# A two-layer decoder trunk: block-inversion products in four runs, bonus sums behind the scores, branch outputs by sequence halves

## The chip, the cores and the metric

The kernel runs on one core of a Trainium2 chip. The metric is the device time of one execution in microseconds (us). Five engines of the core run side by side and meet through semaphores: PE (the matrix engine, TensorE; PEld are its weight loads), DVE (VectorE), ACT (ScalarE), POOL (GpSimd) and SP (SyncE, which issues the DMAs). Each works through its own instructions in the order of the program.

## The reference

Two layers over 1024 tokens of 1024 channels, then a final RMS norm. Each layer does this, in float32:

```python
h = rms_norm(x, norm_g) * (1.0 + scale) + shift        # shift, scale, gate from c
proj = h @ w_in                                         # 1024 -> 8320 columns
pool_u, pool_g, q, k, v, ret_g, rw, rw_g, gate_logits = split(proj)
o_pool = causal_pool_mixer(pool_u, ...) * silu(pool_g)  # windows 2, 4, 8, 16
o_ret  = retention(q, k, v, positions, ...) * silu(ret_g)   # 4 heads, rotary
o_rwkv = rwkv7_time_mix(rw, ...) * silu(rw_g)           # 8 heads of 64, delta rule
y = einsum('btnw,nwd->btnd', stack(o_pool, o_ret, o_rwkv), w_branch)
merged = sum(sigmoid(gate_logits) * y, axis=n)
x = x + gate * (merged @ w_out)
```

The RWKV mixer ends with `y = y + bonus`, where `bonus = sum(r * k * r_k) * v` within a head of 64 channels.

## The kernel before

Activations lie with channels on the 128 partitions and tokens along the free axis, in two halves of 512 tokens. Every large product is made in three matmuls of a reduced-precision float type: each operand x is split into a high part (a copy rounded by ACT, line 562) and a low part (x minus the high part, on POOL, line 563), and `mm3` adds hi·hi, lo·hi and hi·lo into one PSUM tile `acc`. There are three `acc` buffers, two further PSUM buffers of the tag `mx` for all small products, and a double-width PSUM tile `two`.

The weights come as items: `k`, `r`, `v`, `pu`, `rq`, `gate`, `br` (the branch projection), `wg`, `out` and so on. `plan_layer` yields the items in the order in which PE takes them; for each, `wprep` loads two weight tiles `wr` and splits them into `wh` and `wl`. After every dense matmul, `mm1` calls `pump`, which advances the lanes of side work (`norm`, `post`, `rwkv`, `mix`, `ada`) that are due by a clock kept while the program is built: `clock[0]` counts PE's time, `idle_at` the other engines', and a task yields how long it wants to wait. So the place of each small product among the dense ones is settled when the program is built.

One RWKV task (`rwkv_task`) handles two heads on 128 partitions; there are four in a layer, eight in all, and each is called a head here. Its steps:

- `prepare(h)` for each half: decay and key terms (small products `lw`, `nps`), the operand tiles AR and BK, the transposes `vt` of the values into Z, and the bonus: `rkh` and `rkl` are the high and low parts of r·k·r_k, `bon` is their sum over the head by a product with a block matrix of ones, and `bv` is `bon` times v (line 881). `bon` is in a `mx` buffer, which is free again when DVE has formed `bv`.
- `scores(h)`: the transposes `bt` of BK, then the score products `g` (one head in `mx`, one in `two`), masked by DVE into the tile G (line 904).
- `states` and `invert` side by side: the products `av`, and the inversion of 32x32 triangular blocks by forward substitution on DVE, which begins with two transposes (line 928).
- Products of 32x32 blocks that join two inverted blocks into one of 64x64: `m1` and `m2`, each for two quarters q of the units, 16 products a time. Each stands in the profile as 32 matmuls named `m`. They wait for a time by the planner's clock, and between them stand `pace()` and `until(left[q])`.
- Sixteen chunk steps, then a norm; `rwkv_post` writes the result to `od` in DRAM.

Retention (`ret_task`) and pooling (`pool_task`) write their outputs to `od` too. The gate tiles `gsg` that come early are evicted by ACT into tiles of the tag `mo` and stored in `gd`. The rope tables are made once, beside the first head: each half loads the positions, DVE reduces the angle in 12 steps, and ACT takes two sines (lines 299, 300).

The merge: `load_o(n)` loads the outputs of branch n (eight tiles `ol`) and splits them into the single tile `oG` (high parts) and eight tiles `olo` of the tag `mi` (low parts). The tag G of `oG` has one buffer, so the load of a branch waits until the matmuls of the branch before have read theirs. Each `br` item needs all of its branch's tiles; its four products are evicted by DVE and added by DVE or POOL (`mrg`).

Of the kernel before, what the change touches and what calls it, by code (L numbers as in the profile page):

```python
# [19 lines left out]
T = 1024  # L20
# [46 lines left out]
def GT(n, *ds):  # L67
    return [("gate", n, d) for d in ds]


def BR(n, *ds):
    return [("br", n, d) for d in ds]
# [24 lines left out]
def trunk_kernel(ctx, tc, xT, cvec, pos, vecs, consts, w_ada, w_all, pool_w, lora_w, out):  # L97
# [24 lines left out]
    def slot(tag, n, w=HF):  # L122
        def f(s, dt=F32):
            return tp.tile([P, w], dt, tag=tag, name=nm(s), bufs=n)

        return f

    t_rk = slot("rk", 4)
    t_lt = slot("lt", 4)
    t_ri = slot("ri", 7)  # L130
    t_mi = slot("mi", 8, HF + 16)
    t_mo = slot("mo", 4, HF + 16)
    t_vp = slot("vp", 2)
# [134 lines left out]
    def rope_tables():  # L268
        yield 15000
        MAGIC = 12582912.0  # L270
        TWO_PI = 2.0 * math.pi
        cw, left = [], TWO_PI
        for _ in range(3):
            e = 2.0 ** (math.frexp(left)[1] - 8)
            cw.append(math.floor(left / e) * e)
            left -= cw[-1]
        cw.append(left)
        PI_F = 3.1415925
        for h in range(2):
            s = slice(h * HF, (h + 1) * HF)  # L280
            pi = t_mo("posi", I32)[:, 0:HF]
            tc.keep_in_program_order(nc.sync.dma_start(out=pi, in_=pos[:, s].to_broadcast([P, HF])))
            ang = mo("ang")
            nc.vector.tensor_copy(ang, pi)
            nc.vector.tensor_scalar_mul(ang, ang, cs("freq"))
            n = mo("nrot")
            for big in (4096.0, 1.0):
                nc.vector.tensor_scalar(n, ang, 1.0 / (TWO_PI * big), MAGIC, op0=ALU.mult, op1=ALU.add)
                nc.vector.tensor_scalar_sub(n, n, MAGIC)
                for cc in cw:  # L290
                    nc.vector.scalar_tensor_tensor(ang, n, -cc * big, ang, op0=ALU.mult, op1=ALU.add)
                yield 6000
            m = mo("over")
            nc.vector.tensor_scalar_add(n, ang, math.pi / 2)
            nc.vector.tensor_scalar(m, n, math.pi, -TWO_PI, op0=ALU.is_gt, op1=ALU.mult)
            nc.vector.tensor_tensor(n, n, m, op=ALU.add)
            for a in (n, ang):
                nc.vector.tensor_scalar(a, a, PI_F, -PI_F, op0=ALU.min, op1=ALU.max)
            nc.scalar.activation(n[0:64, :], n[0:64, :], AF.Sin)
# [171 lines left out]
    def plan_layer(l):  # L471
        yield from [("lora",)] + RW(0)
        pools = deque(PL(i) for i in range(4))
        pre = deque(GT(0, *range(8)) + GT(1, 0, 1, 4, 5, 6, 7) + GT(2, 2, 3, 4, 5, 6, 7, 0, 1) + GT(1, 2, 3))
        late = deque([("wg", 0), ("wg", 1), ("wg", 2)])
        done = 0
        while done < 4 or prog.get((l, 3), 0) < 13 or pools or halves[l] < 15:
            if done < 4 and prog.get((l, done), -1) >= 0:
                done += 1
                if done < 4:  # L480
                    yield from RW(done)
                yield from RT(done - 1)
            elif pools and 4 - len(pools) <= done and len(lanes["mix"]) < 2:
                yield from pools.popleft()
            elif pre or late:
                q = late if late and (done == 4 and prog.get((l, 3), -1) >= 0 or not pre) else pre
                it = q.popleft()
                early[l].add(it)
                yield it
            elif pools:  # L490
                yield from pools.popleft()
            elif done < 4:
                done += 1
                if done < 4:
                    yield from RW(done)
                yield from RT(done - 1)
            else:
                break
        yield ("merge",)
        seq = GT(1, 2, 3) + BR(0, 0, 2, 4, 6) + [("wg", 0), ("wg", 1)]  # L500
        seq += GT(1, 0, 1) + BR(1, 0, 2) + GT(1, 4, 5) + BR(1, 4)
        seq += [("wg", 2), ("wg", 3)] + GT(1, 6, 7) + BR(1, 6)
        seq += GT(2, 0, 1) + BR(2, 0) + GT(2, 2, 3) + BR(2, 2) + GT(2, 4, 5, 6, 7) + BR(2, 4, 6)
        yield from [it for it in seq if it not in early[l]]
        for part in range(2 + (l + 1 == L)):
            yield from [("out", d, part) for d in out_order(l, part)]
# [276 lines left out]
    def rwkv_task(l, hp, kT, rT, vp, lt, lw):  # L783
# [14 lines left out]
        bvs = []  # L798

        def prepare(h):  # L800
            cr = slice(8 * h, 8 * h + 8)
# [69 lines left out]
            for par in range(2):  # L871
# [1 line left out]
                    Z[64:128, 8 * h + par : 8 * h + 8 : 2, :],  # L873
                    ps[64 * par : 64 * par + 64, :].rearrange("p (c n) -> p c n", n=P),
                )
            yield wait(rkh, rkl)
            ps = mx("bon")
            mmul(ps, bone, rkh, start=True, stop=False)
            mmul(ps, bone, rkl, start=False, stop=True)
            bv = t_ri("bv")  # L880
            nc.vector.scalar_tensor_tensor(bv, ps, 0.5, vp[h], op0=ALU.mult, op1=ALU.mult)
            bvs.append(bv)
# [3 lines left out]
        def scores(h):  # L886
            yield until(whole[h] + 1000)
            for q in range(2):
                ps = mx("bt")
                c0 = 8 * h + 4 * q  # L890
                for c in range(4):
                    trans(ps[:, c * P : (c + 1) * P], jt(BK, slice(0, P), c0 + c), timed=True)
                nc.scalar.copy(BKt[:, c0 : c0 + 4, :], ps.rearrange("p (c n) -> p c n", n=P))
                yield 1300
            for q in range(2):
                c0 = 8 * h + 4 * q
                gps = [mx("g"), cyt()]
                for j in range(4):
                    for hd in range(2):
                        rows = slice(64 * hd, 64 * hd + 64)  # L900
                        mmul(gps[hd][:, j * P : (j + 1) * P], jt(BK, rows, c0 + j), jt(AR, rows, c0 + j), timed=True)
                for hd in range(2):
                    u0 = 16 * hd + c0
                    nc.vector.tensor_tensor(
                        G[:, u0 : u0 + 4, :], gps[hd].rearrange("p (u n) -> p u n", n=P), rm, op=ALU.mult
                    )
                yield 2600
        yield from prepare(0)
        yield from side(scores(0), prepare(1))
        yield from scores(1)  # L910
# [62 lines left out]
        for q in range(2):  # L973
# [4 lines left out]
            nc.scalar.copy(T1[32:64, q * HF : (q + 1) * HF], ps[32:64, :])  # L978
            left.append(max(whole[1], at(MT)) + 300)
            if q == 0:  # L980
                yield pace()
                back(0)
        for q in range(2):
            yield until(left[q])
            ps = mx("m2")
            for u in range(16):
                uu = 16 * q + u
# [428 lines left out]
    for l in range(L):  # L1416
# [39 lines left out]
        merged = None  # L1456
        gates = {}

        def split_o(G, row, kt, o, h):
            hi = G[:, kt * T + h * HF : kt * T + (h + 1) * HF].bitcast(F32R)  # L1460
            lo = mi("olo").bitcast(F32R)
            split(o, hi, lo)
            row.append((hi, lo))

        def new_o():
            return gtile("oG")

        def load_o(n, res):
            G = new_o()
            for kt in range(4):  # L1470
                row = []
                res.append(row)
                for h in range(2):
                    o = mo("ol")
                    nc.sync.dma_start(out=o, in_=od[l][n, kt, h])
                    split_o(G, row, kt, o, h)
                    yield 1250

        gs_free = [t_ri] * 7 + [t_rk] * 4 + [t_vp] * 2 + [t_cs] * 2
        gs_used = {}  # L1480

        def gate_tile(key):
# [16 lines left out]
        def next_o(n):  # L1499
            nonlocal otask  # L1500
            if n < 3:
                osplit.append([])
                otask = add("norm", load_o(n, osplit[n]))

        osplit = []
        unsplit = deque()
        otask = None
        next_o(0)
        mt = [r8("mrg") for _ in range(4)]
        merged = [[None, None] for _ in range(8)]  # L1510
        while wready[0][0][0] != "out":
# [11 lines left out]
            else:  # L1523
                n, d0 = it[1], it[2]
                assert brs.popleft() == (n, d0)
                finish("norm", otask)
                dh = [(d, h) for d in (d0, d0 + 1) for h in range(2)]
                if n == 2 and d0 == 6:
                    dh = [(d, h) for h in range(2) for d in (d0, d0 + 1)]
                for d, h in dh:  # L1530
                    ps = acc_ps()
                    mm3(ps, ws[d - d0], [osplit[n][k][h] for k in range(4)], True, True)
# [12 lines left out]
                    while unsplit and gleft[l] == 0:  # L1545
# [4 lines left out]
                if d0 == 6:  # L1550
                    next_o(n + 1)
        if l:
            drain("ada")
        for task in gate_ada:
# [160 lines left out]
```

## Time and profile before

| | before |
|---|---|
| time, median of 3 runs (lowest to highest) | 2431.59 us (2431.26 to 2433.96) |
| span of the profiled execution | 2431.3 us |
| DVE, ACT, POOL busy | 54%, 33%, 34% |
| DMA over the span | 218.29 MB in queue q1, 28.5% of 16 engines |
| matmuls of the tile m | 1024 of 13312 |

The profiled execution is one execution. Its own time is its span, 2431.3 us from the first to the last instruction; the three runs lie from 0.04 below to 2.7 us above it. In the views of waits a row names the engine and tile that waited, the line, and whose result ended the wait. In timelines a row gives the start, the time from the first start to the last end, and the number of equal instructions; a dense matmul (128x512) lasts 0.39 us there, but in a steady stream one starts every 0.23 us.

### The profile page before, as it was taken

To read this page: it belongs to the slowest core of one execution; us is meant where nothing else is said; L and a number is where in the kernel's file an instruction comes from. 1 tells how busy PE (TensorE), PEld (TensorE's weight loads), DVE (VectorE), ACT (ScalarE), POOL (GpSimd) and SP (SyncE) were. 2 spreads that over 40 slices of the span, in tenths; PEclk is the share of its full clock that TensorE was granted. 3 is DMA by queue.
4 is the path that set the end of the run, shared out by engine and by line. 5 is a ranking of instruction groups with operands and counts; after the bars stand their busy time and mean duration, and the time that the engine had idled before them with its cause. 6 is when DMAs were issued, how large, how long until landed. Compare 5 with 4: busy or idle time off the path is not lost. (4 is left out here: it accounts for less than half of the span.)

```text
span 2431.3 us, 34768 instructions
## 1 busy us (share of the span) xinstructions
PE 2353.2 (97%) x13312; PEld 1925.5 (79%) x13312; DVE 1313.5 (54%) x2564; ACT 799.9 (33%) x1481; POOL 820.8 (34%) x729
## 2 busy tenths in 40 slices
PE   5989999999999999999999999999999999999998
PEld 4768878878887888777877887888787888878888
DVE  7665477367468542457455646745644674322244
ACT  5542333333234223112453324323322323212243
POOL 4321232232232424364442222323313332455241
PEclk9999999999999999999999999999999999999999
DMA  7132112111213225666431211211211222543152
GB/s 252 49 109 70 40 40 75 53 39 53 67 52 109 75 70 173 190 202 206 153 114 44 79 40 40 83 37 44 67 58 39 67 73 71 186 130 96 52 152 79
DMA packets 122487, 220.51 MB, mean 91 GB/s; under 512 B 13904, under 2 KB 17232, under 8 KB 122320
## 3 DMA queue, kind: packets, MB, share of 16 engines
q1 hardware_dynamic: 122320, 218.29, 28.5%
q8 instruction: 104, 1.70, 0.3%
q14 instruction: 63, 0.52, 0.1%
HBM read 172.89 MB, written 45.35 MB: 90 GB/s over the span
## 5 line engine op out<-in xcount | busy, mean ns | idle before, releaser
L563 POOL TENSOR_TENSOR wl<-wr,wh 128x512 fp32r<-128x512 f32 x342 | 452.5, 1324 | 1150.8 <-ACT wh L562 1082.0
L445 PE MATMUL acc<-hhi,wh 128*128 128x512 f32 x2000 | 808.6, 404 | 9.6 <-ACT gsg L1150 8.2
L445 PE MATMUL acc<-hhi,wl 128*128 128x512 f32 x2000 | 811.4, 406 | 1.5 <-POOL r L1070 1.5
L445 PE MATMUL acc<-hlo,wh 128*128 128x512 f32 x2000 | 809.6, 405 | 0.0
L445 PEld LDWEIGHTS acc<-hhi,wh 128*128 128x128 f32 x2000 | 380.6, 190 | 78.9 <-ACT gsg L1150 9.4
L445 PEld LDWEIGHTS acc<-hhi,wl 128*128 128x128 f32 x2000 | 380.8, 190 | 70.5 <-POOL r L1070 2.0
L445 PEld LDWEIGHTS acc<-hlo,wh 128*128 128x128 f32 x2000 | 380.7, 190 | 66.1 <-issue 0.7
L562 ACT CAST wh<-wr 128x512 fp32r<-128x512 f32 x342 | 211.8, 620 | 619.2 <-PE acc L445 436.4
L445 PE MATMUL acc<-olo,wh 128*128 128x512 f32 x384 | 155.3, 405 | 5.9 <-POOL olo L563 5.9
L445 PE MATMUL acc<-oG,wh 128*128 128x512 f32 x384 | 155.0, 405 | 3.1 <-ACT oG L562 1.7
L445 PE MATMUL acc<-oG,wl 128*128 128x512 f32 x384 | 153.0, 400 | 0.0
L1032 DVE SCALAR_TENSOR_TENSOR S<-ch,pc,SP 64x64 f32<-64x64 f32 x256 | 72.5, 283 | 98.8 <-PE ch L445 96.1
L1020 DVE TENSOR_TENSOR xst<-two,MT 64x128 f32<-64x128 f32 x128 | 37.6, 293 | 157.8 <-PE two L445 143.8
L1008 ACT ACTIVATE SP<-S,pc 128x128 f32<-128x128 f32 x128 | 51.5, 402 | 208.1 <-DVE S L1032 198.0
L445 PEld LDWEIGHTS acc<-olo,wh 128*128 128x128 f32 x384 | 73.9, 192 | 25.3 <-POOL olo L563 8.9
L445 PEld LDWEIGHTS acc<-oG,wh 128*128 128x128 f32 x384 | 73.4, 191 | 22.8 <-ACT oG L562 2.9
L445 PEld LDWEIGHTS acc<-oG,wl 128*128 128x128 f32 x384 | 73.8, 192 | 17.8
L1539 DVE SCALAR_TENSOR_TENSOR gs<-gs,acc 128x512 f32<-128x512 f32 x64 | 43.5, 683 | 78.5 <-PE acc L445 78.5
L939 DVE TENSOR_TENSOR tm<-MT,two 64x30 f32<-64x30 f32 (+14 forms) x240 | 76.5, 319 | 12.9 <-ACT two L932 5.6
L945 DVE TENSOR_TENSOR two<-two,tm 64x30 f32<-64x30 f32 (+14 forms) x240 | 78.9, 329 | 7.3
L1027 DVE COPY Z<-ch 64x128 f32<-64x128 f32 x128 | 36.0, 282 | 82.1 <-PE ch L445 81.6
L1537 DVE SCALAR_TENSOR_TENSOR mrg<-gs,acc 128x512 f32<-128x512 f32 x32 | 22.0, 687 | 107.6 <-PE acc L445 105.4
(287 smaller groups left out, 3690.7 us busy)
## 6 DMA issues: line engine op xcount, KB each, us to landing
wr<-in_w_all SPq DMA_DIRECT2D x364, 256.0 KB, 2.7
gd<-gsg SPq DMA_DIRECT2D x74, 256.0 KB, 2.0
gs<-gd SPq DMA_DIRECT2D x74, 256.0 KB, 2.9
wada<-in_w_ada SPq DMA_DIRECT2D x70, 256.0 KB, 3.2
ol<-od SPq DMA_DIRECT2D x64, 256.0 KB, 3.0
ringG<-in_w_ada SPq DMA_DIRECT2D x26, 256.0 KB, 4.9
x<-in_xT SPq DMA_DIRECT2D x16, 256.0 KB, 4.8
od<-po SPq DMA_DIRECT2D x16, 256.0 KB, 2.0
```

Source lines behind the costliest of these rows:

```text
L445: return nc.tensor.matmul(out, lhsT=lhsT, rhs=rhs, start=start, stop=stop, **kw)
L562: nc.scalar.copy(hi, src)
L563: eng.tensor_tensor(lo, src, hi.bitcast(F32), op=ALU.subtract)
L939: nc.vector.tensor_tensor(pr, L3[:, i + 1 :, i : i + 1].to_broadcast([64, n, i]), M3[:, i : i + 1, 0:i].to_broadcast([64, n, i]), op=ALU.mult,
L945: nc.vector.tensor_tensor(M3[:, i + 1 :, 0:i], M3[:, i + 1 :, 0:i], pr, op=ALU.add)
L1008: nc.scalar.activation(SP, S, AF.Copy, scale=pcc)
L1020: nc.vector.tensor_tensor(xst[0:64, :], cy[64:128, 0:P], AV[:, c * P : (c + 1) * P], op=ALU.add)
L1027: nc.vector.tensor_copy(Z[0:64, c, :], ch[0:64, 0:P])
L1032: nc.vector.scalar_tensor_tensor(Sn[rw, rw], ch[rw, P + 64 * hd : P + 64 * hd + 64], pc[rw, c : c + 1], SP[rw, rw], op0=ALU.mult, op1=ALU.add,
L1537: nc.vector.scalar_tensor_tensor(m, s, 1.0, ps, op0=ALU.add, op1=ALU.mult)
L1539: nc.vector.scalar_tensor_tensor(s, s, 1.0, ps, op0=ALU.add, op1=ALU.mult)
```

## The change

Five edits:

1. The block-inversion products: at least 1500 ns of the planner's clock pass before the second, third and fourth run of 16 products.
2. The bonus: `bon` and `bv` leave `prepare(h)` and become a step of their own at the end of `scores(h)`.
3. The branch outputs are loaded and split by halves of the sequence. Half 0 of branch 0 and half 1 of branch 1 go into 8 tiles of the tag `ri`, half 1 of branch 0 and half 0 of branch 2 into 8 of `mi`, the other two into G. Three halves are asked for as the merge begins, the others when an earlier half has been used; each `br` item now does half 0 of both column tiles first.
4. `ri` has 14 buffers instead of 7 (one fewer goes to gate tiles), the rope tables use it instead of `mo`, and the scratch of dynamic DMAs is set to 1024 to make room.
5. The items wg 2 and wg 3, where they were not taken early, move ahead in the merge.

```diff
-    t_ri = slot("ri", 7)
+    t_ri = slot("ri", 14)
...
-            pi = t_mo("posi", I32)[:, 0:HF]
+            pi = t_ri("posi", I32)
...
-            ang = mo("ang")
+            ang = t_ri("ang")
...
-            n = mo("nrot")
+            n = t_ri("nrot")
...
-            m = mo("over")
+            m = t_ri("over")
...
-        seq += GT(1, 0, 1) + BR(1, 0, 2) + GT(1, 4, 5) + BR(1, 4)
-        seq += [("wg", 2), ("wg", 3)] + GT(1, 6, 7) + BR(1, 6)
+        seq += GT(1, 0, 1) + BR(1, 0) + [("wg", 2), ("wg", 3)] + BR(1, 2) + GT(1, 4, 5) + BR(1, 4)
+        seq += GT(1, 6, 7) + BR(1, 6)
...
-            yield wait(rkh, rkl)
+            rks.append((rkh, rkl))
+
+        def bonus(h):
+            yield wait(*rks[h], spare=500)
             ps = mx("bon")
-            mmul(ps, bone, rkh, start=True, stop=False)
-            mmul(ps, bone, rkl, start=False, stop=True)
+            mmul(ps, bone, rks[h][0], start=True, stop=False)
+            mmul(ps, bone, rks[h][1], start=False, stop=True)
...
                 yield 2600
+            yield from bonus(h)
         yield from prepare(0)
         yield from side(scores(0), prepare(1))
         yield from scores(1)
...
             if q == 0:
-                yield pace()
+                yield max(pace(), 1500.0)
                 back(0)
         for q in range(2):
-            yield until(left[q])
+            yield max(until(left[q]), 1500.0)
...
+        def slots_o(n, h):
+            if (n, h) in ((0, 0), (1, 1)):
+                return [t_ri("oz") for _ in range(8)]
+            if (n, h) in ((0, 1), (2, 0)):
+                return [mi("oy") for _ in range(8)]
+            G = gtile("oG")
+            return [G[:, i * HF : (i + 1) * HF] for i in range(8)]
+
+        def load_o(n, h):
+            at_ = slots_o(n, h)
             for kt in range(4):
...
+                o = mo("ol")
+                nc.sync.dma_start(out=o, in_=od[l][n, kt, h])
+                hi, lo = (x.bitcast(F32R) for x in at_[2 * kt : 2 * kt + 2])
+                split(o, hi, lo)
+                osplit[n][h].append((hi, lo))
+                yield 1250
+
+        gs_free = [t_ri] * 6 + [t_rk] * 4 + [t_vp] * 2 + [t_cs] * 2
...
+        for nh in ((0, 0), (0, 1), (1, 0)):
+            next_o(*nh)
...
-                finish("norm", otask)
...
+                if (n, d0) == (1, 4):
+                    next_o(2, 0)
+                for d, h in [(d, h) for h in range(2) for d in (d0, d0 + 1)]:
+                    finish("norm", otask[n, h])
+                    if d0 == 6 and (d, h) == (d0, 1):
+                        next_o(n + 1, 1)
                     ps = acc_ps()
...
-    nc = bacc.Bacc("TRN2", target_bir_lowering=False, num_devices=1)
+    nc = bacc.Bacc("TRN2", target_bir_lowering=False, num_devices=1, dynamic_dma_scratch_size=1024)
```

The edits also move the planner's clock, so most instructions stand elsewhere among the dense matmuls. Three places follow.

PE at the block-inversion products of the first head of layer 1 (m; the numbers are of tiles), before:

```order
L445 MATMUL acc_11723<-hlo_10216,wh_11621 128x512
L445 MATMUL m_2106_11756<-MT_11425,G_10909 32x32 x16
L445 MATMUL m_2107_11775<-MT_11425,G_10909 32x32 x16
L445 MATMUL acc_11723<-hhi_10215,wl_11622 128x512
L445 MATMUL acc_11723<-hhi_10221,wh_11621 128x512
L445 MATMUL m_2108_11795<-G_10909,MT_11425 32x32 x16
L445 MATMUL m_2109_11813<-G_10909,MT_11425 32x32 x16
L445 MATMUL acc_11723<-hlo_10222,wh_11621 128x512
```

and after:

```order
L445 MATMUL m_2112_11739<-MT_11381,G_10910 32x32 x16
L445 MATMUL acc_11733<-hlo_10199,wh_11630 128x512
L445 MATMUL acc_11733<-hhi_10198,wl_11631 128x512
L445 MATMUL acc_11733<-hhi_10204,wh_11630 128x512
L445 MATMUL acc_11733<-hlo_10205,wh_11630 128x512
L445 MATMUL acc_11733<-hhi_10204,wl_11631 128x512
L445 MATMUL acc_11733<-hhi_10210,wh_11630 128x512
L445 MATMUL acc_11733<-hlo_10211,wh_11630 128x512
L445 MATMUL m_2113_11765<-MT_11381,G_10910 32x32 x16
```

Seven dense matmuls now stand between two runs, in every head; the 16 products of a run are two matmuls each in the profile.

DVE at the end of the scores of the very first head (G, the masked scores; bv, the bonus; STREAM_TRANSPOSE, the start of the inversion), before:

```order
L881 SCALAR_TENSOR_TENSOR bv_1455<-bon_1452,vp_792 128x512
L904 TENSOR_TENSOR G_813<-g_1501,cst 128x512
L904 TENSOR_TENSOR G_813<-two,cst 128x512
L904 TENSOR_TENSOR G_813<-g_1524,cst 128x512
L904 TENSOR_TENSOR G_813<-two,cst 128x512
L928 STREAM_TRANSPOSE MT_1547<-G_813 32x1024 x2
```

and after:

```order
L907 TENSOR_TENSOR G_813<-g_1441,cst 128x512
L907 TENSOR_TENSOR G_813<-two,cst 128x512
L907 TENSOR_TENSOR G_813<-g_1464,cst 128x512
L907 TENSOR_TENSOR G_813<-two,cst 128x512
L932 STREAM_TRANSPOSE MT_1512<-G_813 32x1024 x2
L884 SCALAR_TENSOR_TENSOR bv_1510<-bon_1507,vp_792 128x512
```

The bonus bv moved from ahead of the scores to behind the two transposes; in six of the other seven heads one or two more rows stand between.

ACT at the second sine of the rope tables (nrot; gsg are evictions of gate tiles, Z the copies of vt, BKt those of bt), before:

```order
L872 COPY Z_816<-vt_1185 64x4x128
L299 ACT_TABLE_LOAD
L299 ACTIVATE nrot_998<-nrot_998 64x512
L300 ACTIVATE nrot_998<-ang_995 64x512
L562 CAST pw_1149<-pwraw_1151 128x128
L1150 ACT_TABLE_LOAD
L1150 ACTIVATE gsg_1195<-acc_1103 128x512
L1150 ACTIVATE gsg_1198<-acc_1104 128x512
```

and after:

```order
L896 COPY BKt_815<-bt_1202 128x512
L562 CAST wh_1014<-wr_1016 128x512
L299 ACT_TABLE_LOAD
L299 ACTIVATE nrot_998<-nrot_998 64x512
L300 ACTIVATE nrot_998<-ang_995 64x512
L809 ACT_TABLE_LOAD
L809 ACTIVATE aT_1208<-two,vec_92 128x512
L811 ACTIVATE ksq_1210<-k_696,vec_92 128x512
L1154 ACTIVATE gsg_1228<-acc_1104 128x512
```

One of the two gate evictions moved ahead of the sine, and work of the head's second half (aT, ksq) moved to behind it.

More of the change, by code (lines that the diff above doesn't have):

```diff
@@ L797, in rwkv_task @@
         jt = lambda t, rows, c: t[rows, c, :, :].rearrange("p j t -> p (j t)")
-        bvs = []
+        bvs, rks = [], []
         def prepare(h):
@@ L1457, in trunk_kernel @@
         gates = {}
[L1459 to L1469, printed above, removed]
-            for kt in range(4):
[L1471 to L1479, printed above, removed]
+        def slots_o(n, h):
[7 more added lines that the diff above has]
+            at_ = slots_o(n, h)
+            for kt in range(4):
+                o = mo("ol")
[5 more added lines that the diff above has]
+        gs_free = [t_ri] * 6 + [t_rk] * 4 + [t_vp] * 2 + [t_cs] * 2
         gs_used = {}
@@ L1497, in prefetch, with next_o @@
                             nc.sync.dma_start(out=gate_tile((n, d, h)), in_=gd[n, d, h])
-        def next_o(n):
-            nonlocal otask
+        osplit = [[[], []] for _ in range(3)]
+        unsplit = deque()
+        otask = {}
+        def next_o(n, h):
             if n < 3:
[L1502 to L1508, printed above, removed]
+                otask[n, h] = add("norm", load_o(n, h))
+        for nh in ((0, 0), (0, 1), (1, 0)):
+            next_o(*nh)
         mt = [r8("mrg") for _ in range(4)]
@@ L1525, in trunk_kernel @@
                 assert brs.popleft() == (n, d0)
-                finish("norm", otask)
[L1527 to L1530, printed above, removed]
+                if (n, d0) == (1, 4):
[4 more added lines that the diff above has]
+                        next_o(n + 1, 1)
                     ps = acc_ps()
-                    mm3(ps, ws[d - d0], [osplit[n][k][h] for k in range(4)], True, True)
+                    mm3(ps, ws[d - d0], osplit[n][h], True, True)
                     o = (d % 2) * T + h * HF
@@ L1549, in trunk_kernel @@
                         merged[d_][h_] = (a, b)
-                if d0 == 6:
-                    next_o(n + 1)
         if l:
```

## The prediction

> **What bounds the kernel now.** I read the page first, then the waits of the matrix engine PE, then its clock by windows, then timelines of the places that these named.
>
> ```profile
> span 2431.3 us, 34768 instructions
> PE 2353.2 (97%) x13312; PEld 1925.5 (79%) x13312; DVE 1313.5 (54%) x2564; ACT 799.9 (33%) x1481; POOL 820.8 (34%) x729
> ```
>
> PE is the bound: its work is the same before and after (11162 matmul instructions in both programs), so the time can only change by what PE waits and by how fast it runs. The waits (engine, tile, line; us in total, times, longest) that the change touches:
>
> ```profile
> PE acc L445 <- ACT gsg L1150: 8.2, 3, 5.7
> PE acc L445 <- POOL olo L563: 5.9, 6, 2.1
> ...
> PE bt L451 <- DVE bv L881: 3.0, 3, 1.0
> ...
> PE bon L445 <- POOL rkl L866: 2.5, 3, 0.9
> PE bon L445 <- ACT rkh L864: 2.2, 2, 1.4
> ...
> PE acc L445 <- ACT oG L562: 1.7, 2, 1.0
> ```
>
> They are 23.5 us. The other loss is the clock, which the view of cores gives as a mean and the view of windows by place (PEclk is the column after the engines' busy times):
>
> ```profile
> core 0: 2431.3 us, clock 0.985
> ```
>
> ```profile
> 233.73:240.56 6.83, 6.83 (x35) 5.51 (x32) 0.00 (x0) 1.93 (x4) 1.28 (x1) 0.50 0.23 77
> ...
> 1029.03:1035.86 6.83, 6.21 (x14) 4.25 (x14) 6.66 (x5) 1.85 (x3) 6.83 (x6) 0.50 0.76 226
> 1107.54:1110.95 3.41, 3.41 (x9) 2.66 (x9) 1.96 (x4) 0.00 (x0) 1.42 (x2) 0.50 0.52 151
> 1401.09:1404.50 3.41, 3.41 (x8) 2.71 (x9) 0.00 (x0) 0.57 (x1) 0.00 (x0) 0.50 0.00 0
> ...
> 1797.03:1800.44 3.41, 3.41 (x16) 2.73 (x14) 0.00 (x0) 0.58 (x1) 0.07 (x1) 0.50 0.29 77
> 1998.42:2005.25 6.83, 6.83 (x37) 5.61 (x34) 1.99 (x3) 1.46 (x3) 1.27 (x1) 0.50 0.04 14
> 2158.84:2165.67 6.83, 6.12 (x14) 4.41 (x14) 0.00 (x0) 2.48 (x4) 6.56 (x6) 0.50 0.75 227
> ...
> 534.10:537.51 3.41, 3.41 (x11) 2.46 (x9) 0.88 (x2) 0.59 (x1) 0.10 (x1) 0.50 0.00 0
> ```
>
> A mean of 0.985 over 2431.3 us is 36 us lost. The clock falls to half for 3.41 or 6.83 us at a time. Seven of these drops (four long, three short; the first and last of each are shown) begin at the end of a head's block-inversion products m, of eight heads. How much of the 3.41 us ahead of a drop the products filled, by the same view for the tile m alone:
>
> ```profile
> 428.28:431.69 3.41, 1.89 (x54) 1.78 (x55) 0.58 (x1) 1.00 0.52 196
> 431.69:435.11 3.42, 2.42 (x80) 2.31 (x77) 1.73 (x3) 1.00 0.02 5
> 626.26:629.67 3.41, 2.23 (x65) 2.00 (x63) 1.16 (x2) 1.00 0.23 82
> ...
> 1397.68:1401.09 3.41, 2.81 (x84) 2.59 (x80) 1.36 (x3) 1.00 0.31 82
> ```
>
> The first two rows are the one head after which the clock held (1.89 and 2.42 us of products); after 2.23 and 2.81 it fell. So products of 32x32 seem to count as little work, and the limit lies about 2.2 to 2.4 us in 3.41.
>
> **The products in four runs (A).** The timeline of PE at one head (start us, us):
>
> ```profile
> 1395.53 0.39 PE L445 MATMUL acc<-hhi,wh 128*128 128x512 f32 x1
> 1395.76 0.39 PE L445 MATMUL acc<-hlo,wh 128*128 128x512 f32 x1
> 1396.08 2.21 PE L445 MATMUL m<-MT,G 32*32 32x32 f32 x64
> 1398.21 0.50 PE L445 MATMUL acc<-hhi,wl 128*128 128x512 f32 x1
> 1398.55 0.40 PE L445 MATMUL acc<-hhi,wh 128*128 128x512 f32 x1
> 1398.88 2.21 PE L445 MATMUL m<-G,MT 32*32 32x32 f32 x64
> ...
> 1401.58 0.63 PE L445 MATMUL acc<-hhi,wl 128*128 128x512 f32 x1
> 1402.00 0.63 PE L445 MATMUL acc<-hhi,wh 128*128 128x512 f32 x1
> ```
>
> Before, 64 products, two dense matmuls, 64 products. After, the order has seven dense matmuls after each 32 products: 1.1 us of products, then 7 x 0.23 = 1.6 us. No 3.41 us hold more than one run and 0.7 us of the next, 1.8 us, below the 1.89 that held. So I expect all seven drops gone. At half clock a dense matmul starts every 0.42 us (1401.58, 1402.00) instead of 0.23: the short drop at 1401.09 had 8 of the 3.41 / 0.23 = 14.8 that fit, 1.6 us lost of the 1.7 that half would be. Half of four long and three short is 13.7 + 5.1 = 18.8; at 1.6/1.7 of it 17.6. Against it, each run has two borders: 0.32 us from the last dense start to the first product instead of 0.23, and 0.34 from the first to the second dense one after it, 0.2 in all. Two runs more in eight heads: 3.2. A = -14.4. The chain of a head gets some 5 us longer, which costs nothing while other projection tiles fill PE; they do (two gate tiles more than before are left for the merge). If that cover went, eight times 5 us would be idle.
>
> [...]
>
> **The branch outputs by halves (B).** Before, all eight splits of a branch wait for the one G tile that the branch before still reads, and PE waits for POOL:
>
> ```profile
> 1027.33 10.90 POOL L563 TENSOR_TENSOR olo<-ol,oG 128x512 fp32r<-128x512 f32 x8
> ...
> 1043.23 2.91 POOL L1540 TENSOR_TENSOR mrg<-mrg,gs 128x512 f32<-128x512 f32 x2
> ```
>
> The waits for olo and oG are 7.6 us in eight; each also costs the 0.39 - 0.23 = 0.16 by which matmuls overlap, 1.3. Their three drops: 14 dense matmuls where 29.7 fit, 3.6 us lost, less the idle part (6.83 - 6.21 and 6.83 - 6.12), 3.0 and 2.9; 9 of 14.8 in the short one, 1.3. Together 16.1. After, the first three halves have tiles of their own and load ahead. Each later half has two blocks of 24 matmuls, 11 us, from the release of its tiles to its first use. POOL needs 4 x 1.36 = 5.5 us for its splits, but may have four additions of 1.45 and four weight splits of 1.36 in these 11 us: 16.7 at worst, 5.7 late. I keep 4 of the 16.1: B = -12, bounds -16 and 0.
>
> **The bonus behind the scores (C).** The waits of bon and bt, 7.7 us in eight, with 1.3 for overlap, and the drop at 534.10, half of 3.41: 10.7. New is that the product bon takes one of two PSUM buffers, and the second av product needs it back once DVE has formed bv, which the order now puts behind two transposes. One head before (timeline, and all bv):
>
> ```profile
> 186.86 0.69 DVE L904 TENSOR_TENSOR G<-g,cst 128x512 f32<-128x512 f32 x1 [2.75 <-PE two L445]
> 187.47 0.68 DVE L904 TENSOR_TENSOR G<-two,cst 128x512 f32<-128x512 f32 x1
> 188.18 3.99 DVE L928 STREAM_TRANSPOSE MT<-G 32x1024 f32<-32x1024 f32 x2
> ```
>
> ```profile
> L881 DVE SCALAR_TENSOR_TENSOR bv<-bon,vp x16: 677/691/693, 147.7 to 1935.7; 128x512 f32<-128x512 f32 x16
> ```
>
> ```profile
> 192.59 1.14 PE L445 MATMUL av<-Z,G 64*64 64x64 f32 x16
> ```
>
> bv would end at 188.18 + 3.99 + 0.69 = 192.9; PE comes to its second av at 192.59, and 0.46 later for the two bon products: 193.05. So nothing to a few tenths, more where DVE is behind. I take 0.4 in eight heads, 3, and 1 of the 3.0 for bt kept. C = -6.7, bounds -10.7 and +10 (DVE 2 us behind in every head).
>
> **The rope tables in other tiles (D).** Before, ACT evicts gate tiles gsg into the tag that the rope also used, and behind its sines: 8.2 us in three waits, 0.5 for overlap. The second sine waits for DVE, and that for a DMA whose place in SP's queue stays:
>
> ```profile
> 132.14 0.43 DVE L284 CAST ang<-posi 128x512 f32<-128x512 int32 x1 [6.88 <-DMA posi<-in_pos]
> ```
>
> ```profile
> 142.65 0.39 PE L445 MATMUL bon<-rkl,bone 128*128 128x512 f32 x1
> ```
>
> ```profile
> 145.17 0.63 ACT L299 ACTIVATE nrot<-nrot 64x512 f32<-64x512 f32 x1 [2.86 <-DVE nrot L298]
> ...
> 146.79 1.28 ACT L1150 ACT_TABLE_LOAD   x1
> ```
>
> After, four small steps of the pooling stand inside that DVE chain (up to 0.69 each, about 2), so the sine starts near 147, not 145.2; and ACT has queued behind it two sines (1.3), the table (1.28) and five passes as long as a sine, 0.6 (aT, ksq, a gate, ksh, BKt) on which the norm product nps hangs: it can start near 152.8. PE stood from 142.65 + 0.39 = 143.0 before, and I estimate that it gets to nps at the same time (the two shorter gsg waits, 2.5 in all, gone; about as much of products moved ahead). So 9.8 us of wait for 8.7: D = +1.1, bounds -6 and +5.
>
> The rest goes at nothing: seven more t_ri slots, two gate tiles fewer through DRAM, and the wg item earlier in the merge, which the 48 dense matmuls of the item ahead cover; without them it could cost what the longest olo wait did, 2.1. The smaller DMA scratch touches no queue that the page lists.
>
> Sum: -14.4 - 12 - 6.7 + 1.1 = -32 on the execution's 2431.3. The median of the three runs is 2431.59, 0.3 above: 2399.6.
>
> **The rivals.** *The clock does not care for the spacing.* Then A brings only +3.2: 2399.6 + 17.6 = 2417.2. For it: 2.42 us of products held the clock and 2.23 did not, so something else counts too. Against it: seven of eight. Chance 0.08. *POOL stays the bound at the hand-over of branches*, with four of them now instead of three drops: B = 0, 2411.6. Chance 0.1. *Slower: bv behind the transposes.* Each us that DVE is behind at the last G is a us of PE, eight times, and a wait near 2 us drew a drop (olo's longest, 2.1, ahead of 1107.54; 1.3 to 3 us). With DVE 4 us behind: 8 x (4 + 1.7) = 46 in place of 3: 2399.6 + 43 = 2443. It decides above 3.3 us (8 x 5.0 = 40, the 3 and the 37 to 2436.5). Against it: DVE is busy 54% and stood idle 2.75 us ahead of G at 186.86. Chance 0.04. *Nothing gained*: waits reappear one instruction later, since PE's queue has other producers close behind, 2431 +- 4. Chance 0.04.
>
> **The numbers.** The forecast has 0.74: its own range 2386 to 2410 by the bounds of B, C and D. About 0.2% (4.9 us) is what a measurement of this kernel can tell. Faster: 0.74 + 0.08 + 0.1 = 0.92; same 0.04; slower 0.04. The range 2383 to 2420 takes in the first two rivals and D's gain.
>
> **What would show it.** Right: the windows after m at clock 1.00 and a mean clock of 0.993 or more; no waits for bon or for split branch tiles over 2 us in sum; av's waits under 4 us; one wait near 10 us at about 143 us, now of nps. Wrong: drops still behind the products; nps or av waiting in every head; POOL busy throughout the hand-over with PE waiting for oz or oy.

## The result, and the profile after

| | before | after |
|---|---|---|
| time, median of 12 runs (lowest to highest) | 2431.73 us (2427.86 to 2433.96) | 2433.57 us (2430.52 to 2435.66) |
| ratio, 95% interval | | 1.0007 (0.9998 to 1.0015) |
| span of the profiled execution | 2431.3 us | 2432.3 us |
| mean granted clock of that execution | 0.985 | 0.991 |
| PE idle in it (span less PE busy) | 78.1 us | 84.6 us |

The change altered nothing that can be measured; the forecast was 2399.6 us. The page of after, and its mean clock from the view of cores:

```profile
span 2432.3 us, 34706 instructions
...
PE 2347.7 (97%) x13312; PEld 1921.0 (79%) x13312; DVE 1310.9 (54%) x2564; ACT 800.1 (33%) x1481; POOL 819.3 (34%) x729
```

```profile
core 0: 2432.3 us, clock 0.991
```

The clock rose, to 0.991 here and 0.992 in the mean of the twelve runs, a little short of the 0.993 that the prediction named. PE makes as many matmuls as before and is busy 5.5 us less, but it is idle 6.5 us more. Windows of after (us, busy of PE, PEld, DVE, ACT, POOL, then PEclk): the first and the last of the eight stretches with products m, a half-clock stretch that lies elsewhere, and the two merges.

```profile
220.00:233.00 13.00, 13.00 (x164) 10.31 (x163) 0.00 (x0) 3.32 (x7) 2.52 (x2) 1.00 0.21 62
1991.00:2004.00 13.00, 13.00 (x164) 10.31 (x163) 4.14 (x6) 2.93 (x5) 3.83 (x3) 1.00 0.37 102
728.07:734.90 6.83, 5.98 (x20) 5.11 (x21) 3.42 (x4) 5.28 (x10) 1.96 (x2) 0.50 0.62 191
975.00:1150.00 175.00, 172.47 (x770) 139.44 (x769) 104.33 (x159) 35.59 (x60) 78.25 (x59) 1.00 0.63 198
2118.00:2328.00 210.00, 208.84 (x909) 170.13 (x908) 60.01 (x81) 47.84 (x81) 88.58 (x70) 1.00 0.38 113
```

The merges of before, in the same view:

```profile
978.00:1152.00 174.00, 167.82 (x727) 134.56 (x727) 107.65 (x157) 35.76 (x61) 81.88 (x60) 0.97 0.63 196
2110.00:2327.00 217.00, 214.18 (x913) 172.81 (x912) 60.94 (x81) 49.68 (x85) 92.41 (x73) 0.98 0.37 111
```

No half clock is left behind the products (all eight stretches read 1.00) or in the merges, and PE idles 3.7 us there instead of 9.0. The first merge has 43 more matmuls in 1 us more, 42 of them dense, the second 4 fewer in 7 us less: at 0.23 us each some 15 us saved (estimate). What was saved went elsewhere, as PE's waits in after show (us in total, times, longest):

```profile
PE bt L451 <- ACT Z L872: 10.1, 6, 3.1
PE two L445 <- ACT aT L809: 7.5, 1, 7.5
...
PE nps L445 <- DVE ksl L815: 3.7, 2, 3.2
...
PE rvt L451 <- DVE G L907: 3.3, 2, 1.7
...
PE rot L451 <- DVE yc L709: 2.6, 2, 1.3
...
PE av L445 <- DVE bv L884: 0.9, 1, 0.9
...
PE acc L445 <- POOL oz L563: 0.4, 1, 0.4
...
PE bon L445 <- DVE R L753: 0.2, 1, 0.2
```

The waits of bon, olo, oG and gsg, 20.5 us before, are gone but for 0.6 (in after the split tiles are oz, oy and oG). The largest of the new waits is that of bt, which waits for Z, ACT's copies of vt, in six places. About as much, 11.0 us, is spread over retention's small products and vt, two rows of which are shown (all seven tiles: rvt, rkt, rkv, rs, ro, rot, vt); before, these waited 0.2 us. The timelines of PE and then ACT at the longest wait of bt, ahead of the stretch at 728.07:

```profile
723.90 0.60 PE L451 MATMUL vt<-cst,vp 128*128 128x128 f32 x4
...
725.31 0.50 PE L445 MATMUL acc<-hlo,wh 128*128 128x512 f32 x1
728.92 1.11 PE L451 MATMUL bt<-cst,BK 128*128 128x128 f32 x4 [3.10 <-ACT Z L872]
```

```profile
723.93 0.58 ACT L1116 ACTIVATE silu<-acc 128x512 f32<-128x512 f32 x1
727.05 0.62 ACT L864 CAST rkh<-aT 128x512 fp32r<-128x512 f32 x1 [2.54 <-DVE aT L862]
727.69 1.17 ACT L872 COPY Z<-vt 64x512 f32<-64x512 f32 x2
```

vt, lw (left out here) and bt take turns in the two `mx` buffers, so bt needs the one that vt filled and Z empties. vt is done at 724.5, but ACT comes to Z only at 727.69: ahead of it in ACT's order stands the cast rkh, before which ACT idles 2.54 us for DVE. At all six places rkh stands ahead of Z, and ACT idles 1.74 to 4.70 us for DVE before it. The edit moved the products bon, and left their operand rkh where it was. Before, PE met the same DVE chain at bon, behind fifteen dense matmuls at this place; now it meets it at bt, behind seven rows, by way of ACT's queue.

### The profile page after: what moved, and what is told of

It reads as the page before. It is cut to its first block, busy times and chain, and to the rows that moved or that the text cites. A ratio compares the mean times of both kernels' runs of the same rounds, so it can differ in the third digit from the quotient of the medians.

```text
span 2432.3 us, 34706 instructions
## 1 busy us (share of the span) xinstructions
PE 2347.7 (97%) x13312; PEld 1921.0 (79%) x13312; DVE 1310.9 (54%) x2564; ACT 800.1 (33%) x1481; POOL 819.3 (34%) x729
## 5 line engine op out<-in xcount | busy, mean ns | idle before, releaser
L445 PE MATMUL acc<-oz,wh 128*128 128x512 f32 x256 | 81.3, 397 | 1.8 <-DVE gs L1542 1.5
L445 PE MATMUL acc<-oy,wh 128*128 128x512 f32 x256 | 80.7, 395 | 1.2 <-DVE mrg L1540 0.8
L445 PE MATMUL acc<-oG,wh 128*128 128x512 f32 x256 | 79.7, 393 | 0.6 <-DVE gs L1542 0.6
L235 DVE SCALAR_TENSOR_TENSOR ada_acc<-wada,cact,ada_acc 128x512 f32<-128x512 f32 (+1 forms) x70 | 58.8, 840 | 31.5 <-DMA wada<-in_w_ada 30.7
L575 POOL TENSOR_TENSOR vr<-vr,fixed 128x8 f32<-128x8 f32 (+1 forms) x32 | 43.7, 1366 | 85.9 <-DVE vr L574 56.8
L445 PE MATMUL acc<-mhi,wh 128*128 128x512 f32 (+1 forms) x176 | 65.4, 371 | 0.7 <-DVE xres L1588 0.7
```

The source lines that it names most:

```text
L235: nc.vector.scalar_tensor_tensor(part if kt < NKT - 1 else acc, w, cact[:, kt : kt + 1], part, op0=ALU.mult, op1=ALU.add)
L445: return nc.tensor.matmul(out, lhsT=lhsT, rhs=rhs, start=start, stop=stop, **kw)
L575: nc.gpsimd.tensor_tensor(x, x, mhalf.to_broadcast([P, x.free_size()]), op=ALU.pow)
```

## Experiments

Ratios are to the kernel before on the same chip; us are (ratio - 1) x 2431. The expectations reckon with differences of medians, which come out a little otherwise (after less best: 15.7 us, by the ratios 14.6). Several expectations weigh a *scatter theory*: that any edit which moves the planner's clock shifts the places of all small products, and with them PE's waits.

| kernel | ratio (95%) | us | mean clock of its runs |
|---|---|---|---|
| edit 1 alone (runs) | 0.9998 (0.9988 to 1.0007) | -0.5 | 0.991 |
| edit 2 alone (bonus) | 1.0056 (1.0035 to 1.0078) | +13.6 | 0.983 |
| edits 3, 5 alone (halves) | 1.0019 (1.0007 to 1.0031) | +4.6 | 0.986 |
| edit 4 alone (rope) | 1.0028 (1.0016 to 1.0040) | +6.8 | 0.985 |
| after without the bonus ("best") | 0.9947 (0.9931 to 0.9962) | -12.9 | 0.994 |
| after without the rope edit | 1.0004 (0.9995 to 1.0014) | +1.0 | 0.993 |
| after without both (runs and halves) | 0.9963 (0.9951 to 0.9975) | -9.0 | 0.994 |
| after without the runs | 1.0032 (1.0019 to 1.0046) | +7.8 | 0.985 |
| after, pause ahead of bt | 0.9981 (0.9972 to 0.9990) | -4.6 | 0.993 |
| best, 1000 ns ahead of a run | 0.9987 (0.9977 to 0.9996) | -3.2 | 0.993 |
| best, 2000 ns ahead of a run | 0.9973 (0.9962 to 0.9983) | -6.6 | 0.994 |

**Each edit alone.** The runs:

```diff
-                yield pace()
+                yield max(pace(), 1500.0)
...
-            yield until(left[q])
+            yield max(until(left[q]), 1500.0)
```

> The kernel before with edit 1 alone (at least 1500 ns of the planner's clock ahead of the second, third and fourth run of products). Three theories are told apart by the first four runs. Bonus theory: A and B are real, about -12 each, and the gain is given back in the heads by edit 2, since bt now stands directly behind vt and waits for ACT's copies Z. Rope theory: the same, but the rope tables (edit 4) give it back. Scatter theory: any edit that moves the planner's clock shifts the places of all small products, and with them the waits of PE in the heads by 10 us or more either way, so that a gain in one place is lost in others. Here the bonus and rope theories expect no drop of the clock behind the products m, waits of PE in the heads within 4 us of before, and 2418 to 2420 us. The scatter theory expects the drops gone too, but waits that have changed by 10 us or more, so a time anywhere from 2410 to 2432.

The bonus:

```diff
+        def bonus(h):
+            yield wait(*rks[h], spare=500)
             ps = mx("bon")
...
                 yield 2600
+            yield from bonus(h)
```

> The kernel before with edit 2 alone (bon and bv behind the scores). Bonus theory: bon's waits go (about -5), bt waits for Z by 8 to 12 us, further waits and drops come with it: 2436 to 2445 us. Rope theory: near my term C, 2425 us (-6.7). Scatter theory: no wait for Z in particular; the waits change at many tiles, 2422 to 2442 us.

The halves (slots_o and load_o(n, h) of the change, with ri of 14 buffers and the smaller scratch):

```diff
-        next_o(0)
+        for nh in ((0, 0), (0, 1), (1, 0)):
+            next_o(*nh)
```

> The kernel before with the branch outputs by halves (edits 3 and 5, and the larger ri with the smaller scratch; the rope tables stay in mo). Bonus and rope theories: the waits for oG and olo and the drops of the merges go, the heads of layer 0, which stand ahead of the first merge, are as before within 3 us: 2418 to 2421 us. Scatter theory: the merges gain about 13 and heads or gates lose part of it: 2418 to 2432 us.

The rope tables (posi, nrot and over likewise; with ri of 14 buffers and the smaller scratch):

```diff
-            ang = mo("ang")
+            ang = t_ri("ang")
...
```

> The kernel before with the rope tables in tiles of the tag ri alone (and the larger ri with the smaller scratch). Rope theory: the wait behind the second sine is 7 us or more for one tile, a drop of about 10 us of half clock follows, and it costs 10 us or more: 2441 us or above. Bonus theory: within 3 us of my term D (+1), 2430 to 2436 us. Scatter theory: 2422 to 2442 us, with changes far from the rope tables as well.

The bonus came out in the range that its theory named, with bt's new wait, somewhat shorter than the 8 to 12 us expected:

```profile
PE bt L451 <- ACT Z L872: 6.7, 6, 2.0
```

The runs took half clock away (mean clock 0.986 to 0.991, some 12 us) and gained nothing; halves and rope came out slower. Runs and rope lie in the ranges of the scatter theory, halves just above all that were named. The four sum to +24.5, and all together to +1.7: they don't add from this starting point.

**One edit taken back.**

```diff
 after without the bonus:
+            yield wait(rkh, rkl)
+            ps = mx("bon")
...
-            yield from bonus(h)
 after without the rope edit:
-            ang = t_ri("ang")
+            ang = mo("ang")
...
 after without the runs:
-                yield max(pace(), 1500.0)
+                yield pace()
...
```

> The kernel after with edit 2 undone (bon and bv in prepare again). By themselves the edits came to -0.8 (runs), +15.0 (bonus), +4.5 (halves) and +7.8 us (rope), together +26.5, but all of them to +1.8. Two theories for that. Clock theory: every edit that shifts products makes PE wait at new places, and the half-clock stretches behind m and behind these waits take what is saved; with the products in four runs the heads are nearly free of them, so the rest costs less beside edit 1 than alone. Scatter theory: the waits move by 5 to 10 us either way with every edit, and no sum holds. Here the bonus must be most of the loss by the clock theory: 2420 to 2426 us, no wait of bt for Z. Scatter theory: within 5 us of after, either way.

> The kernel after with the rope tables back in tiles of the tag mo. Rope alone cost 7.8 us. Clock theory: the wait of 7.5 us for aT and the 10.2 us of half clock behind it go, but gsg waits come back: 2426 to 2431 us. Scatter theory: within 5 us of after, either way.

> The kernel after with the bonus and the rope tables undone: the runs and the halves together (my terms A and B). Clock theory: the drops behind m and in the merges are gone together, waits in the heads near before: 2415 to 2422 us, the best of all. Scatter theory: 2428 to 2436 us, the sum of the two alone (-0.8 and +4.5).

> The kernel after with edit 1 undone (the products m in two pairs of runs again). Clock theory: the half-clock stretches behind m are back in most heads, about 12 us of loss: 2443 to 2449 us, mean clock near 0.984. Scatter theory: 2428 to 2440 us.

With the bonus back the kernel beats both before and after: 2417.88 us (median of 4), faster than expected. Runs and halves alone gave 2422.77, just above the range of the clock theory. Without the runs the kernel took 2438.79 us, less than that theory's range and within the scatter theory's: the runs are worth 6.1 us here (1.0032 to 1.0007), not 12. With the rope edit taken back it took 2431.88 us, by the ratios 0.7 less than after, which is within the noise; without the bonus the rope edit gains 3.9 us (0.9963 to 0.9947), and these intervals overlap too. In the best kernel bt waits for Z nowhere, but 4.6 us for DVE's rsm, a tile of retention, and the merges wait for other things than before:

```profile
PE acc L445 <- DVE gs L1538: 4.9, 5, 1.6
PE acc L445 <- POOL wl L563: 4.5, 4, 2.0
```

gs is DVE's eviction of the branch products and wl POOL's split of the weights.

**The wait for Z itself.**

```diff
-            yield until(whole[h] + 1000)
+            yield max(until(whole[h] + 1000), 2500.0)
```

> The kernel after with a pause of 2500 ns of the planner's clock ahead of bt, so that twelve dense matmuls instead of seven stand between vt and bt. Undoing the bonus edit gave 15.7 us of time back. Bonus theory: what costs is the place of bt directly behind vt, where it waits for ACT's copies Z, and the half-clock stretches behind these waits. Then bt's waits for Z (10.1 us) fall under 3 us, the drops at 332, 728 and 1312 us go, and the time is 2420 to 2426 us, the rest of the 15.7 being the borders of the bonus products, which now stand alone (16 x 0.2 = 3.2 us). Rival: the cost lies in the new place of bon and bv and in the later work that they delay; then bt's waits go, but others grow, and the time is within 4 us of after.

2425.22 us, 6.3 below after by the ratios. bt still waits for Z, but less:

```profile
PE bt L451 <- ACT Z L872: 4.4, 2, 3.5
```

More dense matmuls ahead of bt, with bon still in its new place, give nearly half of the 14.6 back, though not all went as expected: bt still waits 4.4 us where I said under 3, and the mean clock rose only from 0.992 to 0.993. Whether the three half-clock stretches went is not shown. The rival, within 4 us of after, is not borne out. bt's wait thus seems a good part of the bonus cost, but the pause moves the plan too, so the share is rough, as the last group of runs will show.

**The spacing, and a second profile of before.**

```diff
-                yield max(pace(), 1500.0)
+                yield max(pace(), 1000.0)
...
```

> The best kernel so far (after with the bonus back) with 1000 instead of 1500 ns ahead of each run of products: five dense matmuls instead of seven between runs, so 3.41 us hold up to 2.1 us of products. By the limit of about 2.2 us that I read from before, the clock holds behind m and the time is 2417 to 2420 us; if the limit is lower, some of the eight heads show half clock again and it is 2420 to 2428 us. By the scatter theory, which makes the gain of 13.6 us a lucky draw of the planner, it is anywhere from 2418 to 2432 us, with other waits at many places.

The other with 2000.0 in its place:

> The same with 2000 ns: nine dense matmuls between runs, 3.41 us hold at most 1.3 us of products. Direct theory: no half clock behind m, 2416 to 2421 us. Scatter theory: 2418 to 2432 us.

> The kernel before, for a second profile. If the half-clock stretches begin on a fixed grid of 3.41 us whose phase against the program differs from one execution to the next, some heads that lost the clock for 6.83 us in the first profile will lose it for 3.41 or not at all, and others more; the waits stay within 1 us. If the phase is fixed, the same stretches stand at the same places.

At five dense matmuls between runs the mean clock was 0.993. Two stretches of 3.41 us with 2.12 us of products, tile m alone (in this view PE, PEld and ACT, then PEclk):

```profile
232.46:235.87 3.41, 2.12 (x64) 2.01 (x64) 0.58 (x1) 1.00 0.28 82
2014.22:2017.63 3.41, 2.12 (x62) 2.01 (x63) 0.58 (x1) 1.00 0.00 0
```

Behind the first of them the clock held (all engines):

```profile
235.87:239.28 3.41, 3.41 (x21) 2.84 (x18) 0.25 (x1) 0.58 (x1) 0.00 (x0) 1.00 0.00 0
```

So nothing here speaks against the limit of about 2.2 us that I had read from the first profile of before, where the clock fell after 2.23. Yet 1000, 1500 and 2000 ns gave 2428.23, 2417.88 and 2425.11 us, at mean clocks of 0.993, 0.994 and 0.994: something else moves times by 10 us. The second profile of before lost the clock at all eight heads, also at the second, which had held it in the first (the stretch with the tile m alone, then the one behind it with all engines):

```profile
430.78:434.19 3.41, 3.00 (x96) 2.89 (x95) 1.52 (x3) 1.00 0.08 32
```

```profile
434.20:437.61 3.41, 3.41 (x10) 2.62 (x9) 0.00 (x0) 1.31 (x3) 1.28 (x1) 0.50 0.08 28
```

**Edits that change nothing but the plan.** Two pauses of the planner were made 100 ns longer, in each of the three kernels:

```diff
 first null edit, behind each pair of score products:
-                yield 2600
+                yield 2700
 second null edit, behind each set of transposes bt, and one step of retention:
-                yield 1300
+                yield 1400
```

> A null edit of the kernel before: the pause of the planner behind each pair of score products is 2700 instead of 2600 ns. It removes and adds no instruction; it only moves the places of side work by a fraction of a dense matmul's slot, and of everything that is planned after. Scatter theory: time moves by up to 5 us either way from 2431 us (2425 to 2437), by waits in the heads. Direct theory, by which the sizes found for edits 1, 3 and 4 (from +7 to -14 us for one edit, depending on which others stand beside it) are true interplay of these edits: within 1.5 us of before.

> Another null edit of the kernel before: 1400 instead of 1300 ns behind each set of four transposes bt, and behind a like step of retention. The same two theories: within 5 us either way (scatter), or within 1.5 us (direct).

> The first null edit on the best kernel so far (after with the bonus back, 13.6 us faster than before). Scatter theory: part of the 13.6 was a lucky draw of places; 2418 to 2428 us. Direct theory: 2417 to 2420 us.

> The second null edit on the best kernel so far. Scatter theory: 2418 to 2428 us; direct theory: 2417 to 2420 us. With n3 and the two other spacings (2428.2 and 2425.1 us) it gives the middle of the draws for edits 1, 3, 4 and 5 without the bonus; by both theories all of them stay below the kernel before, and after (2433.6) stays above them.

> The first null edit on the kernel after, so that each version has the same three draws of the planner. From before to the best kernel (edits 1, 3, 4, 5) the ratios moved by -0.53%, -0.73% and -0.55% in the three draws, -14.7 us in the mean. By the bonus theory edit 2 costs about as much in each draw: after stands 7 to 18 us above the best kernel of the same draw, here 2428 to 2439 us. By the rival, that the bonus cost is itself a draw, after is within 4 us of the best kernel in at least one of the draws: here 2417 to 2425 us.

> The second null edit on the kernel after. Bonus theory: 7 to 18 us above the best kernel of the same draw (2426.7), 2434 to 2445 us. Rival: within 4 us of it, 2423 to 2431 us.

| | before | best | after | edits 1, 3, 4, 5 | edit 2 |
|---|---|---|---|---|---|
| as they stand | 1 | 0.9947 (0.9931 to 0.9962) | 1.0007 (0.9998 to 1.0015) | -0.53% | +0.60% |
| 2700 ns | 1.0031 (1.0018 to 1.0043) | 0.9958 (0.9943 to 0.9973) | 0.9999 (0.9989 to 1.0009) | -0.73% | +0.41% |
| 1400 ns | 1.0032 (1.0019 to 1.0045) | 0.9977 (0.9968 to 0.9986) | 1.0019 (1.0010 to 1.0029) | -0.55% | +0.42% |

A null edit makes the kernel before 7.5 and 7.8 us slower, a wider margin than expected. I call the places that a plan happens to give a draw: of three draws, before as it stands is the best. (A row of the table is one and the same pause, not the same places in each kernel.) Over the three draws the edits hold their worth: 1, 3, 4 and 5 gain 0.60% in the mean, 14.7 us, and edit 2 costs 0.48%, 11.6 us, so that all five together gain some 3 us instead of nothing. The rival, that the bonus cost is itself a draw, is not borne out: it is there three times out of three, with bt's wait for Z (10.1 us as they stand, 10.0 and then, in the 1400 ns draw of after:)

```profile
PE bt L451 <- ACT Z L872: 13.3, 6, 3.7
```

PE's busy and idle time by the pages (span less busy), best to after: busy +10.7, +6.5 and -1.2 us, idle +4.2, +5.9 and +13.6. bt waited in the best kernel as well, 5.5, 7.4 and 2.7 us in the three draws and mostly for rsm, so of the 10.1, 10.0 and 13.3 us only 4.6, 2.6 and 10.6 are new. The mean clock of the runs fell too, from 0.994 to 0.992, 0.992 and 0.991, worth at most some 5, 6 and 7 us. The cost is waits and half clock, in changing shares.

## Why the prediction was wrong

The forecast was A - 14.4, B - 12, C - 6.7, D + 1.1. Measured in the plans as they stand: A, B and D together -12.9 instead of -25.3, C +14.6 instead of -6.7. Of the 34 us between forecast and result 21 are C and 12 the other three.

- **C failed: it is the term whose sign came out wrong.** I priced what bon's removal frees, and the second av, which was right (0.9 us of waits, 3 allowed). The failed step is "1 of the 3.0 for bt kept": I took bt's new place as free, and bt waited 10.1 us. I did not ask what stands ahead of Z in ACT's order, namely rkh with its wait for DVE. That is the rival "waits reappear one instruction later", to which I gave 0.04. The 3.2 us of borders of the moved bon, which an expectation above reckons with, are not there: bon is a 128x512 product like the dense ones, and in after it starts 0.23 us behind the matmul ahead of it in 13 of 16 places. How the 14.6 us divide is known only roughly: part is bt's wait, part half clock. Casting rkh behind Z would take DVE's chain out of bt's way; it was not tried.
- **A was right in its mechanism and too large in its worth.** All drops behind m went (1.00 at all eight heads of after). Against -14.4 the runs brought -0.5 alone, -6.1 in after (1.0032 to 1.0007) and -13.6 beside the halves (1.0019 to 0.9963). One part is the count: the drops of one profile are a sample, and the runs of edit 1 alone lose only 12 us less to half clock on average (0.986 to 0.991), not 18.8. The other is the draw of places; in edit 1 alone PE waits more at nps (before: 2.9 us for ksl and 0.8 for G):

```profile
PE nps L445 <- DVE ksl L815: 6.2, 4, 3.2
...
PE nps L445 <- DVE G L904: 2.5, 3, 1.0
```

The null edit of before, which has no spacing, shows the same two rows:

```profile
PE nps L445 <- DVE ksl L815: 4.8, 3, 3.2
...
PE nps L445 <- DVE G L904: 3.8, 4, 1.4
```

So a change of draw alone brings such waits; that the spacing itself brings none was not shown.
- **B was right in the merges themselves.** Tiles oz and oy wait 0.4 us in all of after, so the rival "POOL stays the bound" falls, the merges keep the full clock, 3.7 us of idle time are left where the sum kept 4 in all, and the merges saved some 15 us (the estimate above) where the sum had 12. In the best kernel the same merges idle more; its windows:

```profile
987.00:1148.00 161.00, 152.11 (x674) 121.90 (x673) 96.64 (x152) 32.97 (x57) 75.87 (x57) 1.00 0.67 209
2125.00:2312.00 187.00, 187.00 (x816) 152.67 (x815) 59.47 (x80) 42.13 (x71) 80.06 (x64) 1.00 0.40 123
```

They idle 8.9 us, all in the first, for DVE's gs and POOL's wl. Counted like those of after, they save some 9 us, 53 matmuls fewer in 13 us less and 97 fewer in 30 (estimate). So most of what A, B and D lack in the best kernel was lost outside the merges. Over the whole kernel halves alone lost 4.6 us and halves beside the runs gained 8.5 (0.9998 to 0.9963): by the null edits, draws move a kernel by nearly as much.
- **D's number came out, in part by luck.** I expected one wait of 9.8 us, and the norm products nps at 152.8; they begin at 152.34. But PE waits 7.5 us, and not at nps: it stops earlier, at a score product that needs the PSUM tile `two`, which ACT empties (aT) behind the second sine and a table load. ACT, then PE:

```profile
146.41 0.63 ACT L299 ACTIVATE nrot<-nrot 64x512 f32<-64x512 f32 x1 [4.88 <-DVE nrot L298]
147.06 0.63 ACT L300 ACTIVATE nrot<-ang 64x512 f32<-64x512 f32 x1
147.70 1.28 ACT L809 ACT_TABLE_LOAD   x1
149.00 0.69 ACT L809 ACTIVATE aT<-two,vec 128x512 f32<-128x512 f32 x1
```

```profile
149.74 0.58 PE L445 MATMUL two<-AR,BK 64*128 64x128 f32 x1 [7.53 <-ACT aT L809]
...
152.34 0.63 PE L445 MATMUL nps<-ksh,bone 128*128 128x512 f32 x1
```

In after the edit costs 0.7 us (1.0004 to 1.0007), where I said 1.1, but alone it cost 6.8 and without the bonus it gained 3.9; its own worth is not told apart from the draw.
- **A term was missing.** Every edit here moves most rows of a plan, and the plan of before is the best of three draws: null edits cost 7.5 and 7.8 us. My sum took all waits that I did not name as unchanged. The waits of retention's products and vt show that they are not: 0.2 us before, 11.0 in after, 6.3 in the best kernel, 3.0 in the 1400 ns draw of after. What stays open is which of the many moved places make a draw good; the pages show that both busy and idle time of PE differ.

The rival "the clock does not care" falls (no drop behind m in eight heads), and "slower: bv behind the transposes" too: av waited 0.9 us.

## What to carry to other kernels

When a product is moved away, its operands' makers stay behind in their engines' queues: list what now stands ahead of the next thing that PE needs, on every engine, and look for an instruction there that itself waits. Where a planner places side work, run null edits first: they tell the size of effect that one edit must pass, and whether the kernel before is a good draw; an edit is then judged over several draws. Half-clock stretches of one profile are a sample (before lost the clock at seven heads in one execution, at eight in another), so their cost is taken from the mean clock of several runs.

## What the runs showed of the hardware

Half-clock stretches begin on a grid of 3.413 us whose place against the program differed between two executions: in the first profile of before the starts 233.73 and 1998.42 are 517 steps apart, in the second 236.22 and 434.20 are 58, but the second grid lies 2.49 us later against the program. The first execution lost the clock at seven heads, the second at all eight. In the first profile of before and in that of after, with each one's grid laid from its first drop, I summed the time of the products m in every step at full clock that held over 0.9 us of them. In before there are 14 such steps: the six with at most 1.89 us and one with 2.42 were followed by full clock, one with 2.23 and the six with 2.47 to 2.82 by half clock. In after there are 25, with 1.19 to 1.67 us, and none was followed by half clock. PE counted as busy for 3.41 us in every one of these steps, so here a busy PE alone did not keep the clock. What else the clock follows, no run here takes apart.
